# Convolution taps and modulation multiplies change places in a two-layer fp32 block on one core

## The chip, the core and the metric

One core of a Trainium2 chip runs the whole program. The metric is the device time in microseconds (us) of one execution. The engines are named as in the profile: PE (TensorE, matrix products; PEld its weight loads), DVE (VectorE), ACT (ScalarE), POOL (GpSimd) and SP (SyncE, which issues every DMA of this kernel).

## The reference

Two layers of a block with three parallel branches are computed in fp32 for 512 tokens of width 1024 and 256 context tokens; layer 1 gives the 512 tokens only.

```
mod = silu(c) @ w_mod[l] + b_mod[l]                # 6 x 1024 per token kind: sh1 sc1 g1 sh2 sc2 g2
u = x * (1 + sc1) + sh1                            # same for the context with its own columns
a, qkv, o_pre, g_if, cq, ckv, kr, gates = split(u @ w_in + b_in)
conv:   h = val * sigmoid(gate); h = depthwise_conv(h, 31 taps) + b_dw
        y_a = silu(layer_norm(h)) @ w_conv_out
mLSTM:  bidirectional chunkwise recurrence over q, k, v with gate rows g_if
        y_b = (sigmoid(o_pre) * norm(h)) @ w_mlstm_out
MLA:    attention over latent q, k, v          y_c = o @ w_mla_out
y = (g_a * y_a + g_b * y_b + g_c * y_c) @ w_out + b_out        # g_i = sigmoid(gates)
x = layer_norm(alpha * x + g1 * y)
x = layer_norm(alpha * x + g2 * (relu(u2 @ w1 + b1)^2 @ w2 + b2))      # u2 = x*(1+sc2)+sh2
```

## The kernel before

**Products.** Activations lie feature-major: 8 tiles of 128 features by T = 768 columns (512 tokens, then 256 context tokens). Each fp32 product is three float32r products, since every operand is split in a high and a low part: `wh` by `uh` (L266), `wh` by `ul` (L267) and `wl` by `uh` (L268). `gemm` makes 128 output features: 8 feature tiles by 3 matmuls over 512 columns, and the same again over the 256 of the context where they are needed (layer 0, and the keys of both layers). `win` does this for a tile of `w_in`. The PSUM tile `pg` has two buffers, `pt` four.

**Weights.** `plan` lists the weight tiles in the order of use, and `wget` keeps two tiles staged ahead. `wload` (L257 to L262) loads a tile of 512 KB into `wr`, ACT casts it to `wh` (L261), and `wl` = `wr` − `wh` is made by DVE, or by POOL for the 24 gate tiles and the 4 output gate tiles of a layer (L262). Each of the three has three buffers.

**Order of a layer.** Convolution input (4 pairs of products, value and gate, giving `hc`, L490); values with gate rows and rope keys by tokens (12 products in two halves; DVE adds the bias into `vt` L540, `gt` L543 and `kr`); the gate-row chain (ACT and DVE on 36 rows, L562 to L611), whose results PE transposes in four steps (L619) and two small products (L628); keys and queries (4 + 4 products); the mLSTM; 24 gate products, which go to DRAM (`z_dram`); 4 output gate products; the merges 0 and 1 of the branches (8 products each, reading `z_dram` back); latent products, attention, merge 2 with output projection, first norm, MLP, second norm.

**Two kinds of DVE work are spread over these products.** Python generators issue them step by step.

- `mod_pieces(l, r)` is a third of a layer's modulation. For each of 4 groups and 8 feature tiles it loads 256 KB of `w_mod` into `wm` and multiplies it into two accumulators `mda` (first tile L163, the others L165: two DVE instructions per load); then PE sums over the partitions (L173), ACT copies (L176), PE transposes (L178), DVE adds the bias (L181). `pull(k)` takes k steps. Layer 0's first third has its own code ahead of the layers; the other two are 64 steps, 128 multiplies, pulled in layer 0 beside the convolution input, values, keys and queries. Layer 1's modulation runs in layer 0's MLP and is not touched: in layer 1 the `pull`s named here find nothing left.
- `conv_taps` is the depthwise convolution: for each of 4 tiles one opening TENSOR_SCALAR (L500), then 30 steps that each add one shifted, scaled copy of `hc` to `ca` (L506). A step is one instruction over about 512 columns and, in layer 0, a second over about 256: 240 tap instructions in layer 0, 120 in layer 1. `some_taps(k)` takes k steps. Six steps are asked for after each gate product, and ahead of the convolution's layer norm, at gate product 20 in layer 0 and 21 in layer 1, the rest:

```
for b in range(3):
    for mt in range(8):
        g = gate(b, mt)
        nc.sync.dma_start(z_dram[b, mt, :, :n], g[:, :n])
        some_taps(6)
        if b * 8 + mt == (20 if l == 0 else 21):
            some_taps(200)
            ln_fm(ca, 4, groups, conv_emit)
```

`ln_fm` transposes `ca` on PE (L314), takes statistics on DVE (L315, L318) and POOL (L321), and writes the convolution's activation `sa`, which merge 0 needs.

**What sets the order.** A scheduler takes the program in the order in which it is written as a priority and fixes one static order of instructions for each engine; it may take an instruction of lower priority early where an engine would be free by its own estimate. So the taps of the text after gate products begin to run in the mLSTM. All DMAs go through SP's one queue. The tiles `wm`, `mda`, the mLSTM's `dm` and `kw`, the layer norm's `ln`, `th`, `y` and the merges' `ml` share one pool (`mw`) of 8 buffers.

Of the kernel before, what the change touches and what calls it, by code (L numbers as in the profile page):

```python
# [11 lines left out]
AF = mybir.ActivationFunctionType  # L12
# [32 lines left out]
def build(tc, I, out):  # L45
# [64 lines left out]
    # silu of the conditioning vectors, as 32 stationary columns (two of them used)  # L110
# [12 lines left out]
    def first_mod(q):  # L123
        """shift and scale of the first layer's input for 256 features"""
        wv = I["w_mod"][0].rearrange("(k p) (s q c) -> p k s q c", p=128, s=6, q=4)
        ws = []
        for k in range(8):
            w = wtile("wm")
            ws.append(w)
            nc.sync.dma_start(w.rearrange("p (s c) -> p s c", s=2), wv[:, k, 0:2, q, :])  # L130
            if not q and k == 3:
                nc.sync.dma_start(cst[:, 0:128], I["consts"][:, 0:128])
                nc.sync.dma_start(cols[0], I["cols"][0])
        yield
        ps = pt()
        for k, w in enumerate(ws):
            for t in range(4):
                PE.matmul(ps[32 * t:32 * t + 32, :128], sil[:, k, :], w[:, t * 128:(t + 1) * 128],
                          start=(k == 0), stop=(k == 7), tile_position=(0, 32 * t))
            yield  # L140
        rows = small(128, "modrows", 1)
        A.copy(rows, ps[:, :128])
        p2 = pt()
        PE.transpose(p2[:, :128], rows, ident)
        o = OFF["b_mod"]
        V.tensor_tensor(MC[0][:, 0:16, :].rearrange("p (s q t) v -> p s q t v", s=2, q=4)[:, :, q],
                        p2[:, :128].rearrange("p (s t j) -> p s t j", s=2, t=2)[:, :, :, 0:2],
                        cols[0][:, o:o + 16].rearrange("p (s q t o) -> p s q t o", s=2, q=4, o=1)[:, :, q]
                        .to_broadcast([128, 2, 2, 2]), op=OP.add)

    def mod_pieces(l, r):
        """a third of a layer's modulation: products on VectorE, paced by the matrix products, sums over
        the partitions on TensorE; the last layer's norms and gates have no context tokens"""
        nv = 1 if (l == L - 1 and r) else 2
        for g in range(4):
            av = [wtile("mda") for _ in range(nv)]
            for k in range(8):
                w = wtile("wm")
                c0 = r * 2048 + g * 512
                nc.sync.dma_start(w, I["w_mod"][l, k * 128:(k + 1) * 128, c0:c0 + 512])  # L160
                for v in range(nv):
                    if k == 0:
                        ins = V.tensor_scalar(av[v], w, sil[:, k, v:v + 1], None, op0=OP.mult)  # L163
                    else:
                        ins = V.scalar_tensor_tensor(av[v], w, sil[:, k, v:v + 1], av[v], op0=OP.mult, op1=OP.add)  # L165
                    if v == 0:
                        tc.add_manual_dep(ins.ins, mark[0].ins.name, NOSYNC)
                if k % 2 or l == 0:
                    yield
            ps = pt()  # L170
            for v in range(nv):
                for t in range(4):
                    PE.matmul(ps[32 * t:32 * t + 32, :128], pick[:, v, :], av[v][:, t * 128:(t + 1) * 128],  # L173
                              start=(v == 0), stop=(v == nv - 1), tile_position=(0, 32 * t))
            rows = small(128, "modrows", 1)
            A.copy(rows, ps[:, :128])  # L176
            p2 = pt()
            PE.transpose(p2[:, :128], rows, ident)  # L178
            i0 = r * 16 + 4 * g
            o = OFF["b_mod"] + i0  # L180
            V.tensor_tensor(MC[l][:, i0:i0 + 4, 0:nv],  # L181
                            p2[:, :128].rearrange("p (t j) -> p t j", t=4)[:, :, 0:nv],
                            cols[l][:, o:o + 4].rearrange("p (t o) -> p t o", o=1).to_broadcast([128, 4, nv]),
                            op=OP.add)
# [8 lines left out]
    def affine(l, name, g, b, sc, sh):  # L193
        """columns of (n*g + b)*(1 + sc) + sh = n*P + Q"""
# [6 lines left out]
    def plan():  # L201
        """the staged weights, in the order of their use"""
# [73 lines left out]
    # the last matrix product so far  # L276
    mark = [None]

    def gemm(w, koff, nk, act, spec):
        """psum[128 features, tokens]; w: (hi, lo) staged tiles with k tiles of 128 columns from koff;  # L280
        spec: number of tokens, or (first token, last, psum column) triples"""
# [10 lines left out]
    def gemm_parts(w, nk, act, spec):  # L292
        """as gemm, with sums of their own for every range of tokens: [(first token, last, psum)]"""
# [10 lines left out]
    def ln_groups(src, nk, groups, emit, base=0):  # L304
        """layer norm over the features of feature-major tiles; emit(k, first column, columns, psum)"""
# [50 lines left out]
    # ---------------------------------------------------------------- first modulation  # L356
# [27 lines left out]
    def first_w(j):  # L384
        """weights and sums of one of the first three products, which run along with the loads of the modulation"""
# [67 lines left out]
    for l in range(L):  # L453
# [5 lines left out]
        # token groups that follow each other through the norms: (tiles, modulation column, first token, last)  # L459
# [14 lines left out]
        # ------------------------------------------------------------ conv input  # L474
# [6 lines left out]

        for j in range(4):
            val, tg = slot("val"), slot("tg")
            for c0, c1, ps in conv_in(MT_VAL + j):
                A.activation(val[:, c0:c1], ps, AF.Identity, bias=HB(MT_VAL + j), scale=0.5)
            for c0, c1, ps in conv_in(MT_GATE + j):
                A.activation(tg[:, c0:c1], ps, AF.Tanh, bias=HB(MT_GATE + j), scale=0.5)
            pull(3)
            h = slot("hc")
            V.scalar_tensor_tensor(h[:, :n], tg[:, :n], 1.0, val[:, :n], op0=OP.add, op1=OP.mult)  # L490
            hc.append(h)
            pull(3)
# [17 lines left out]
        taps = conv_taps()  # L510
# [5 lines left out]
        # ------------------------------------------------------------ values, gates and rope keys, by tokens  # L516
# [8 lines left out]
        for hf, w_n in ((0, VG0), (1, VG1)):  # L525
            ws = [wget("w_vg", l, hf * 2 + q) for q in range(2)]
            for tt in range(NT):
# [10 lines left out]
                pull(1)  # L538
# [10 lines left out]
        # ------------------------------------------------------------ gate rows: heads forward at 0-3, backward at 32-35  # L549
# [64 lines left out]
        A.activation(E_, m, AF.Exp, scale=-1.0)  # L614
        kinds = {}
# [15 lines left out]
        # ------------------------------------------------------------ keys, queries  # L631
        kT, qT = [], []
        for h in range(MH):
            ps = win(MT_K + h, T)
            t = slot("kT")
            A.activation(t, ps, AF.Identity, bias=kb[l][:, h:h + 1], scale=KSCALE)
            kT.append(t)
            pull(4)
        for h in range(MH):
# [4 lines left out]
            pull(4)  # L644
        pull(99)

        # ------------------------------------------------------------ mLSTM
# [8 lines left out]
        def weights_of(tt, ds):  # L656
            """scores of a chunk times their decays, keys on partitions, for the directions ds"""
# [98 lines left out]
        # ------------------------------------------------------------ merges: (tanh(gate/2) + 1) * y  # L756
# [19 lines left out]
        for b in range(3):  # L776
            for mt in range(8):
                g = gate(b, mt)
                nc.sync.dma_start(z_dram[b, mt, :, :n], g[:, :n])
                some_taps(6)  # L780
                if b * 8 + mt == (20 if l == 0 else 21):
# [3 lines left out]
        # ------------------------------------------------------------ output gate of the mLSTM  # L785
        ot = []
        for h in range(MH):
# [3 lines left out]
            ot.append(t)  # L791

        def merge(b, wname, act):
            for mp2 in range(4):
                w = wget(wname, l, mp2)
                for i in range(2):
                    mt = 2 * mp2 + i
                    ps = gemm(w, 4 * i, 4, act, n)
                    for c0, c1 in segs:
# [5 lines left out]
                        nc.sync.dma_start(z_dram[b, mt, :, c0:c1], g)  # L805

        # gated, normalised mLSTM output
# [12 lines left out]
        merge(1, "w_mo", ht)  # L820

        # ------------------------------------------------------------ latent queries, keys and values
# [27 lines left out]
        def rope(x, tt, nh):  # L850
            """x: [128, nh, 32], in place"""
# [12 lines left out]
        # ------------------------------------------------------------ attention  # L864
# [164 lines left out]
        # ------------------------------------------------------------ columns of the norms and gates  # L1029
# [10 lines left out]
        # ------------------------------------------------------------ merge of the third branch, output projection  # L1040
        def packed(m):
            """m f32r tiles of 256 columns, three to a slot"""
# [22 lines left out]
        # ------------------------------------------------------------ first norm  # L1065
# [15 lines left out]
        def residual(v, c0, c1):  # L1081
            """alpha * x + g1 * b_out, two feature tiles of 256 tokens to a tile"""
# [22 lines left out]
        # ------------------------------------------------------------ MLP  # L1105
# [37 lines left out]
        # ------------------------------------------------------------ second norm  # L1143
# [49 lines left out]
def _kmaj(w, m):  # L1193
    """[K, M] -> [M/m, 128, K/128 * m]"""
# [95 lines left out]
```

## Time and profile before

| | |
|---|---|
| median of 3 runs | 2622.0 us (2621.68 to 2622.0) |
| span of the profiled execution | 2620.9 us, 38348 instructions |
| PE busy | 2482.4 us, 95% of the span |
| DVE busy | 1609.0 us, 61% |
| ACT busy | 940.4 us, 36% |
| POOL busy | 381.9 us, 15% |

No time outside the span is given for the profiled execution; its span is 1.1 us below the median of the runs. Busy times of several engines overlap. Only what keeps PE idle, or slows its clock, and what lies at the two ends lengthens a program in which PE is 95% busy: 138.5 us of the span are idle on PE. A line of the waits gives engine, tile and line that waited, then engine, tile and line that ended the wait, the sum in us, how many times, and the longest. A row of windows gives the stretch in us from the start, its length, each engine's busy time with its number of instructions, the granted clock of PE (1.00 is full speed), the share of the DMA engines and GB/s. A row of single instructions has start, duration, engine, line, operation and tiles; in brackets the time that the engine sat idle before, and who ended that.

### The profile page before, as it was taken

To read this page: it belongs to the slowest core of one execution; us is meant where nothing else is said; L and a number is where in the kernel's file an instruction comes from. 1 tells how busy PE (TensorE), PEld (TensorE's weight loads), DVE (VectorE), ACT (ScalarE), POOL (GpSimd) and SP (SyncE) were. 2 spreads that over 40 slices of the span, in tenths; PEclk is the share of its full clock that TensorE was granted. 3 is DMA by queue.
4 is the path that set the end of the run, shared out by engine and by line. 5 is a ranking of instruction groups with operands and counts; after the bars stand their busy time and mean duration, and the time that the engine had idled before them with its cause. 6 is when DMAs were issued, how large, how long until landed. Compare 5 with 4: busy or idle time off the path is not lost. (4 is left out here: it accounts for less than half of the span.)

```text
span 2620.9 us, 38348 instructions
## 1 busy us (share of the span) xinstructions
PE 2482.4 (95%) x15272; PEld 2172.9 (83%) x15272; DVE 1609.0 (61%) x2847; ACT 940.4 (36%) x1607; POOL 381.9 (15%) x235
## 2 busy tenths in 40 slices
PE   7999976999999999999999999999599999999998
PEld 5888865888897899888888989778488888988887
DVE  4887999333256777655554473489954567645456
ACT  3133311321457563222222252333133575532323
POOL 0002278303000021000000040025212000200002
PEclk9999988999999999999999999999799999999999
DMA  8543221446110554343332242224254206333333
GB/s 293 177 138 108 79 78 49 128 141 219 61 41 1 174 172 141 120 130 129 118 119 74 61 147 70 73 89 137 81 176 161 62 4 191 117 96 94 96 97 113
DMA packets 137236, 298.46 MB, mean 114 GB/s; under 512 B 13776, under 2 KB 55248, under 8 KB 137056
## 3 DMA queue, kind: packets, MB, share of 16 engines
q1 hardware_dynamic: 137056, 296.00, 35.7%
q8 instruction: 120, 1.97, 0.3%
q14 instruction: 60, 0.49, 0.1%
HBM read 265.49 MB, written 30.46 MB: 113 GB/s over the span
## 5 line engine op out<-in xcount | busy, mean ns | idle before, releaser
L261 ACT CAST wh<-wr 128x1024 fp32r<-128x1024 f32 (+1 forms) x328 | 345.6, 1055 | 1223.4 <-PE pg L267 917.7
L262 DVE TENSOR_TENSOR wl<-wr,wh 128x1024 fp32r<-128x1024 f32 (+2 forms) x272 | 340.9, 1254 | 427.0 <-ACT wh L261 423.4
L268 PE MATMUL pg<-uh,wl 128*128 128x512 f32 (+1 forms) x1280 | 457.8, 358 | 32.4 <-POOL wl L262 32.4
L266 PE MATMUL pg<-uh,wh 128*128 128x512 f32 (+1 forms) x1280 | 460.0, 359 | 1.2 <-ACT gt__17652 L760 1.2
L267 PE MATMUL pg<-ul,wh 128*128 128x512 f32 (+1 forms) x1280 | 458.7, 358 | 0.6 <-POOL ul L1167 0.6
L262 POOL TENSOR_TENSOR wl<-wr,wh 128x1024 fp32r<-128x1024 f32 x56 | 226.4, 4048 | 519.9 <-ACT wh L261 510.0
L268 PEld LDWEIGHTS pg<-uh,wl 128*128 128x128 f32 x1280 | 246.0, 192 | 65.6 <-POOL wl L262 33.7
L266 PE MATMUL pg<-hidh,wh 128*128 128x512 f32 (+1 forms) x832 | 285.8, 345 | 3.9 <-DVE mv L318 2.0
L267 PE MATMUL pg<-hidl,wh 128*128 128x512 f32 (+1 forms) x832 | 285.4, 343 | 0.0
L268 PE MATMUL pg<-hidh,wl 128*128 128x512 f32 (+1 forms) x832 | 284.4, 342 | 0.0
L266 PEld LDWEIGHTS pg<-uh,wh 128*128 128x128 f32 x1280 | 246.7, 193 | 35.5 <-ACT gt__17652 L760 1.4
L267 PEld LDWEIGHTS pg<-ul,wh 128*128 128x128 f32 x1280 | 246.3, 192 | 33.4 <-POOL ul L1167 1.1
L506 DVE SCALAR_TENSOR_TENSOR ca<-hc,cols,ca 128x511 f32<-128x511 f32 (+10 forms) x360 | 252.7, 753 | 2.4
L321 POOL TENSOR_TENSOR rs<-rs,mhalf 128x1 f32<-128x1 f32 x30 | 24.4, 819 | 1331.8 <-DVE rs L320 1299.2
L267 PE MATMUL pg<-u2l,wh 128*128 128x512 f32 (+1 forms) x608 | 210.1, 347 | 0.3 <-POOL u2l L1078 0.2
L268 PE MATMUL pg<-u2h,wl 128*128 128x512 f32 (+1 forms) x608 | 209.9, 346 | 0.0
L266 PE MATMUL pg<-u2h,wh 128*128 128x512 f32 (+1 forms) x608 | 209.7, 347 | 0.0
L1135 DVE SCALAR_TENSOR_TENSOR acc<-pg,mod,acc 128x512 f32<-128x512 f32 (+1 forms) x168 | 106.0, 659 | 168.6 <-PE pg L268 168.6
L266 PEld LDWEIGHTS pg<-hidh,wh 128*128 128x128 f32 x832 | 157.7, 190 | 25.4 <-issue 3.6
L267 PEld LDWEIGHTS pg<-hidl,wh 128*128 128x128 f32 x832 | 158.4, 190 | 18.9 <-DVE hidl L1125 1.6
L268 PEld LDWEIGHTS pg<-hidh,wl 128*128 128x128 f32 x832 | 158.1, 190 | 18.0
L165 DVE SCALAR_TENSOR_TENSOR mda<-wm,sil,mda 128x512 f32<-128x512 f32 x224 | 161.9, 748 | 3.8 <-DMA wm<-w_mod 2.2
(359 smaller groups left out, 4766.5 us busy)
## 6 DMA issues: line engine op xcount, KB each, us to landing
wr<-w SPq DMA_DIRECT2D x140, 512.0 KB, 3.6
wr<-w_in_fm SPq DMA_DIRECT2D x104, 512.0 KB, 3.6
wm<-w_mod SPq DMA_DIRECT2D x192, 256.0 KB, 4.6
wr<-w_out SPq DMA_DIRECT2D x40, 512.0 KB, 3.6
ml<-z_dram SPq DMA_DIRECT2D x104, 128.0 KB, 2.8
ml<-z_dram SPq DMA_DIRECT2D x48, 256.0 KB, 3.8
z_dram<-ml SPq DMA_DIRECT2D x32, 256.0 KB, 4.1
dm<-m_dram SPq DMA_DIRECT2D x20, 256.0 KB, 5.0
```

Source lines behind the costliest of these rows:

```text
L165: ins = V.scalar_tensor_tensor(av[v], w, sil[:, k, v:v + 1], av[v], op0=OP.mult, op1=OP.add)
L261: A.copy(h[:, :n], r[:, :n])
L262: eng.tensor_sub(lo[:, :n], r[:, :n], h[:, :n])
L266: PE.matmul(ps, hs, xh, start=first, stop=False)
L267: PE.matmul(ps, hs, xl, start=False, stop=False)
L268: return PE.matmul(ps, ls, xh, start=False, stop=last)
L321: G.tensor_tensor(rs[:, 0:1], rs[:, 0:1], mhalf[:, 0:1], op=OP.pow)
L506: V.scalar_tensor_tensor(acc[:, a:b], h[:, a + d:b + d], wd(15 + d), acc[:, a:b], op0=OP.mult, op1=OP.add)
L1135: V.scalar_tensor_tensor(acc[mt][:, c0:c1], ps[:, c0:c1], mc[:, 40 + mt, v:v + 1], acc[mt][:, c0:c1], op0=OP.mult, op1=OP.add)
```

## The change

Taps move from the gate products to the stages ahead of the mLSTM, the modulation from there to the gate products, the output gate and the merges. The generator `conv_taps` is defined ahead of the convolution input and created after the first `hc`. The key products with their code move ahead of the transposes of the gate rows. The layer norm of the convolution comes at gate product 10 in both layers. Comments and docstrings are taken out. After the change the lines are: opener L488, taps L494, `hc` L511, `vt` L541, `gt` L544, `kr` L548, gate-row transposes L628, the two small products L637.

```
 # convolution input, per pair of products
-            pull(3)
             h = slot("hc")
             V.scalar_tensor_tensor(h[:, :n], tg[:, :n], 1.0, val[:, :n], op0=OP.add, op1=OP.mult)
             hc.append(h)
-            pull(3)
+            if j == 0:
+                taps = conv_taps()
+            some_taps(9)
 # values, per product
-                pull(1)
+                some_taps(2)
 # keys: moved from behind the loop over `kinds` (the transposes) to ahead of it
+        for h in range(MH):
+            ps = win(MT_K + h, T)
+            t = slot("kT")
+            A.activation(t, ps, AF.Identity, bias=kb[l][:, h:h + 1], scale=KSCALE)
+            kT.append(t)
+            some_taps(4)
         kinds = {}
...
-            kT.append(t)
-            pull(4)
 # queries
             qT.append(t)
-            pull(4)
-        pull(99)
+            some_taps(5)
 # gates
-                some_taps(6)
-                if b * 8 + mt == (20 if l == 0 else 21):
+                some_taps(3)
+                pull(2)
+                if b * 8 + mt == 10:
                     some_taps(200)
                     ln_fm(ca, 4, groups, conv_emit)
 # output gate, per product
             ot.append(t)
+            pull(2)
 # merge, per product
                         nc.sync.dma_start(z_dram[b, mt, :, c0:c1], g)
+                    pull(2)
...
         merge(1, "w_mo", ht)
+        pull(99)
```

The static order shows where the steps end up. In the rows the names are tiles; a row is line, operation, output and inputs, and the size.

DVE in layer 0's gate stage before the change, in the middle of the taps (`ca` gets a scaled `hc`):

```order
L506 SCALAR_TENSOR_TENSOR ca<-hc,cols_82,ca 128x497
L506 SCALAR_TENSOR_TENSOR ca<-hc,cols_82,ca 128x241
L500 TENSOR_SCALAR ca<-hc,cols_82 128x768
L506 SCALAR_TENSOR_TENSOR ca<-hc,cols_82,ca 128x511
L506 SCALAR_TENSOR_TENSOR ca<-hc,cols_82,ca 128x255
```

DVE after the change, from the last mLSTM rows on into the gate stage (`mda` accumulates the modulation, `mod_99` receives its sums):

```order
L748 TENSOR_SCALAR hacc<-hacc,mmv,mrs 128x128 x4
L165 SCALAR_TENSOR_TENSOR mda<-wm,sil,mda 128x512 x10
L163 TENSOR_SCALAR mda<-wm,sil 128x512 x2
L494 SCALAR_TENSOR_TENSOR ca<-hc,cols_82,ca 128x242
L181 TENSOR_TENSOR mod_99<-pt,cols_82 128x8
L494 SCALAR_TENSOR_TENSOR ca<-hc,cols_82,ca 128x497
L494 SCALAR_TENSOR_TENSOR ca<-hc,cols_82,ca 128x241
L494 SCALAR_TENSOR_TENSOR ca<-hc,cols_82,ca 128x497
L494 SCALAR_TENSOR_TENSOR ca<-hc,cols_82,ca 128x241
L165 SCALAR_TENSOR_TENSOR mda<-wm,sil,mda 128x512 x14
L163 TENSOR_SCALAR mda<-wm,sil 128x512 x2
```

Before, 211 of layer 0's tap instructions stood behind the last mLSTM row, next to each other; now five are left there, among groups of 14 modulation multiplies. Ahead of that row stand 235 taps instead of 29, and 6 modulation multiplies instead of 128.

DVE at the first value products of layer 0 before the change:

```order
L490 SCALAR_TENSOR_TENSOR hc<-tg,val 128x768
L165 SCALAR_TENSOR_TENSOR mda<-wm,sil,mda 128x512
L163 TENSOR_SCALAR mda<-wm,sil 128x512
L165 SCALAR_TENSOR_TENSOR mda<-wm,sil,mda 128x512
L163 TENSOR_SCALAR mda<-wm,sil 128x512
L165 SCALAR_TENSOR_TENSOR mda<-wm,sil,mda 128x512
L540 TENSOR_TENSOR vt<-pg,bvg_596 128x2x128
L543 TENSOR_TENSOR gt<-pg,bvg_596 128x4x4
L540 TENSOR_TENSOR vt<-pg,bvg_596 128x2x128
L543 TENSOR_TENSOR gt<-pg,bvg_596 128x4x4
```

The same place after the change:

```order
L511 SCALAR_TENSOR_TENSOR hc<-tg,val 128x768
L488 TENSOR_SCALAR ca<-hc,cols_82 128x768
L541 TENSOR_TENSOR vt<-pg,bvg_596 128x2x128
L494 SCALAR_TENSOR_TENSOR ca<-hc,cols_82,ca 128x511
L494 SCALAR_TENSOR_TENSOR ca<-hc,cols_82,ca 128x255
```

and 12 taps further on:

```order
L494 SCALAR_TENSOR_TENSOR ca<-hc,cols_82,ca 128x508
L494 SCALAR_TENSOR_TENSOR ca<-hc,cols_82,ca 128x252
L544 TENSOR_TENSOR gt<-pg,bvg_596 128x4x4
L494 SCALAR_TENSOR_TENSOR ca<-hc,cols_82,ca 128x507
L494 SCALAR_TENSOR_TENSOR ca<-hc,cols_82,ca 128x251
L494 SCALAR_TENSOR_TENSOR ca<-hc,cols_82,ca 128x507
L494 SCALAR_TENSOR_TENSOR ca<-hc,cols_82,ca 128x251
L541 TENSOR_TENSOR vt<-pg,bvg_596 128x2x128
L544 TENSOR_TENSOR gt<-pg,bvg_596 128x4x4
```

The two additions that read the first value product stood side by side; now 16 tap instructions stand between them, and four ahead of the second product's.

PE in layer 0's keys before the change (the numbers tell buffers apart; `pg_1670` is the second key product, `cst` holds the identity):

```order
L267 MATMUL pg_1670<-ul_171,wh_1279 128x256
L268 MATMUL pg_1670<-uh_170,wl_1280 128x256
L619 MATMUL pt_1544<-cst_78,rows_1485 128x36 x6
L266 MATMUL pg_1670<-uh_178,wh_1279 128x256
L267 MATMUL pg_1670<-ul_179,wh_1279 128x256
```

and after it (`pg_1661` is the fourth key product, `pg_1773` the first query product):

```order
L267 MATMUL pg_1661<-ul_474,wh_1527 128x256
L268 MATMUL pg_1661<-uh_473,wl_1528 128x256
L628 MATMUL pt_1720<-cst_78,rows_1399 128x36 x6
L628 MATMUL pt_1730<-cst_78,lf_1410 128x36 x6
L628 MATMUL pt_1740<-cst_78,ndr_1416 128x36 x6
L628 MATMUL pt_1750<-cst_78,lnr_1414 128x36 x6
L266 MATMUL pg_1773<-uh_170,wh_1592 128x512
```

The first transposes of the gate rows, which need the end of the gate-row chain on DVE, stood inside the second key product; now all four follow the fourth. The split of the fourth key product's weights stands on DVE behind that chain.

More of the change, by code (lines that the diff above doesn't have):

```diff
@@ L480, in conv_in @@
             return [(0, n, win(i, n)[:, :n])]
[L482 to L487, printed above, removed]
-            pull(3)
-            h = slot("hc")
-            V.scalar_tensor_tensor(h[:, :n], tg[:, :n], 1.0, val[:, :n], op0=OP.add, op1=OP.mult)
-            hc.append(h)
-            pull(3)
         def conv_taps():
@@ L508, in conv_taps @@
                     yield
-        taps = conv_taps()
+        taps = None
         def some_taps(k):
@@ L514, in some_taps @@
                 next(taps, None)
+        for j in range(4):
+            val, tg = slot("val"), slot("tg")
+            for c0, c1, ps in conv_in(MT_VAL + j):
+                A.activation(val[:, c0:c1], ps, AF.Identity, bias=HB(MT_VAL + j), scale=0.5)
+            for c0, c1, ps in conv_in(MT_GATE + j):
+                A.activation(tg[:, c0:c1], ps, AF.Tanh, bias=HB(MT_GATE + j), scale=0.5)
+            h = slot("hc")
+            V.scalar_tensor_tensor(h[:, :n], tg[:, :n], 1.0, val[:, :n], op0=OP.add, op1=OP.mult)
+            hc.append(h)
+            if j == 0:
+                taps = conv_taps()
+            some_taps(9)
         vt = []
@@ L614, in build @@
         A.activation(E_, m, AF.Exp, scale=-1.0)
+        kT, qT = [], []
+        for h in range(MH):
[4 more added lines that the diff above has]
+            some_taps(4)
         kinds = {}
@@ L629, in build @@
             V.tensor_copy(ast[:, d].rearrange("p t h -> p (t h)"), ps[:, :NT * 4])
[L632 to L636, printed above, removed]
-            kT.append(t)
-            pull(4)
         for h in range(MH):
```

## The prediction, made before the changed kernel was run

> **What bounds the kernel now.** I began with the page's forty slices, which show where TensorE (PE) is not full.
>
> ```profile
> PE   7999976999999999999999999999599999999998
> DVE  4887999333256777655554473489954567645456
> POOL 0002278303000021000000040025212000200002
> PEclk9999988999999999999999999999799999999999
> GB/s 293 177 138 108 79 78 49 128 141 219 61 41 1 174 172 141 120 130 129 118 119 74 61 147 70 73 89 137 81 176 161 62 4 191 117 96 94 96 97 113
> ```
>
> A slice is 65.5 us. PE bounds the kernel almost everywhere; the holes are slices 6 and 7 (327 to 459 us, layer 0's gate products) and slice 29 (1835 to 1900 us, the same stage of layer 1), where VectorE (DVE) is full and the granted clock drops. The list of PE's waits names who ended them:
>
> ```profile
> PE pt L314 <- DVE ca L506: 37.1, 3, 22.8
> PE pg L268 <- POOL wl L262: 32.4, 3, 11.5
> PE pt L619 <- DVE rows L591: 9.6, 2, 4.9
> ```
>
> (us, times, longest.) PE waits 37.1 us for the last convolution taps in front of the convolution's layer norm, 32.4 us for gate weights whose low part GpSimd (POOL) splits off, and twice 4.8 us in the keys for the gate-row chain. The table by stage puts these on the clock:
>
> ```profile
> core 0: us, PE busy (x) PEld busy (x) DVE busy (x) ACT busy (x) POOL busy (x), PEclk, DMA share, GB/s
> 57.30:101.90 44.60, 43.98 (x277) 37.44 (x276) 35.92 (x53) 9.59 (x13) 0.00 (x0) 1.00 0.66 215
> 101.90:142.00 40.10, 39.32 (x324) 38.37 (x323) 32.86 (x83) 5.75 (x7) 0.00 (x0) 1.00 0.45 145
> 142.00:224.80 82.80, 77.72 (x496) 66.62 (x495) 65.67 (x107) 28.17 (x47) 5.88 (x3) 0.96 0.44 141
> 224.80:309.20 84.40, 78.19 (x551) 70.22 (x551) 77.52 (x209) 31.05 (x88) 15.20 (x9) 1.00 0.27 82
> 309.20:468.20 159.00, 121.89 (x656) 105.70 (x656) 144.33 (x263) 24.04 (x26) 120.69 (x15) 0.87 0.24 76
> 543.00:640.00 97.00, 97.00 (x565) 85.80 (x564) 43.50 (x60) 19.57 (x21) 18.85 (x16) 1.00 0.64 206
> 1637.40:1712.30 74.90, 70.03 (x389) 60.08 (x388) 32.78 (x56) 24.15 (x35) 7.15 (x3) 0.98 0.28 82
> 1712.30:1771.00 58.70, 52.81 (x336) 46.41 (x335) 52.20 (x130) 25.34 (x72) 10.89 (x5) 0.97 0.24 76
> 1771.00:1863.60 92.60, 92.60 (x410) 76.61 (x409) 89.39 (x110) 27.84 (x34) 48.25 (x20) 1.00 0.44 140
> 1863.60:1905.00 41.40, 9.05 (x48) 7.71 (x47) 35.69 (x57) 4.78 (x7) 4.61 (x5) 0.63 0.09 30
> ```
>
> Rows one to five are layer 0: convolution input, values, keys with queries, mLSTM, and gates up to the layer norm. Row six is the merges. The other four are layer 1's keys with queries, its mLSTM, its gates, full, and its layer norm, nearly empty: 41.40 − 9.05 = 32.35 us idle. In row five 159.00 − 121.89 = 37.1 us are idle, namely the 32.4 on POOL and 4.74 on the taps (37.1 − 32.35).
>
> Why POOL is late there:
>
> ```profile
> 354.58 26.82 POOL L262 TENSOR_TENSOR wl<-wr,wh 128x1024 fp32r<-128x1024 f32 x1 [6.54 <-ACT wh L261]
> 486.05 2.40 POOL L262 TENSOR_TENSOR wl<-wr,wh 128x1024 fp32r<-128x1024 f32 x1 [5.94 <-ACT wh L261]
> 1815.78 2.58 POOL L262 TENSOR_TENSOR wl<-wr,wh 128x1024 fp32r<-128x1024 f32 x1 [2.42 <-ACT wh L261]
> L506 DVE SCALAR_TENSOR_TENSOR ca<-hc,cols,ca 128x507 f32<-128x507 f32 (+22 forms) x43 | 22.3, 590 | 0.0
> L506 DVE SCALAR_TENSOR_TENSOR ca<-hc,cols,ca 128x497 f32<-128x497 f32 (+14 forms) x30 | 22.2, 743 | 1.0
> L165 DVE SCALAR_TENSOR_TENSOR mda<-wm,sil,mda 128x512 f32<-128x512 f32 x14 | 9.4, 743 | 0.0
> ```
>
> The same split takes 2.40 us where no taps run (second row), 26.82 us in the midst of layer 0's taps (first), and 2.58 us in the midst of layer 1's (third). Layer 0's taps come in pairs on separate columns (512 and 256), and 43 of 590 ns mean fit into 22.3 us: they overlap, 0.52 us each. Layer 1's each need the one before, 30 in 22.2 us with 1.0 us of gaps, and there POOL gets in. The Trainium skill (page "SBUF — State Buffer", section "SBUF: two separate sides") says that a VectorE operation with two SBUF inputs and a GpSimd operation that reads SBUF take turns on a shared port, each locking it for one whole instruction. By it alone a split would wait for one tap, 0.75 us at most; layer 1's 2.58 us agrees, layer 0's 26.82 us does not, so the measurement decides. By the page the first rival below could not happen and the sum would stand as it is; by the first row it keeps its chance.
>
> **The change, part by part.** Of 120 tap steps per layer 96 move ahead of the mLSTM; layer 0's 64 modulation steps (128 DVE instructions) move behind it.
>
> *Layer 0's gate stage.* No run of paired taps is left there, so 32.4 and 4.74 us of waiting go. A stalled product also restarts slowly:
>
> ```profile
> 353.40:361.75 8.35, 8.35 (x50) 7.39 (x50) 8.35 (x17) 1.85 (x2) 7.17 (x1) 1.00 0.12 47
> 370.01:388.11 18.10, 7.28 (x28) 5.61 (x27) 18.07 (x23) 1.85 (x2) 16.84 (x3) 0.72 0.31 80
> 381.46 0.80 PE L268 MATMUL pg<-uh,wl 128*128 128x512 f32 x1 [10.82 <-POOL wl L262]
> 382.05 0.63 PE L266 MATMUL pg<-uh,wh 128*128 128x512 f32 x1
> 382.48 0.63 PE L267 MATMUL pg<-ul,wh 128*128 128x512 f32 x1
> ```
>
> Behind the 10.82 us wait matmuls start 0.43 us apart, where layer 1's gates have 92.60 / 410 = 0.226. 24 of 512 columns take 5.4 us; the second row has 7.28 busy, so about 1.8 us per stall, 7.3 for the four. From above, 656 matmuls at 8.35 / 50 are 109.6 us against 121.89 busy: 12.3. Between 7.3 and 12.3 I take 9. Gain 37.1 + 9 = **46.1** (44.4 to 49.4).
>
> The modulation's multiplies that now stand there overlap too: 14 in 9.4 us (last row above), 0.67 each. A group of 16 could keep a split out for about 9.4 + 2.4 = 12 us. What a split may take before PE waits is 26.82 − 10.82 = 16 us, so I cost it at nothing; if two groups merge, see the first rival.
>
> *Layer 1's layer norm* waits for nothing any more: in the new order its last tap stands inside the mLSTM. Gain 32.35, and 2 for the clock (0.63 over 9.05 us would give 3.3): **34.3**.
>
> *Keys ahead of the gate-row transposes.* The four transposes now follow all four key products, so L619's 4.74 us and the restart (PEclk 0.96 over 77.72 us bounds it at 3.1; I take 1.5) go: 4.74 is 9.6 less layer 1's 74.90 − 70.03 = 4.87. Late next is the fourth key product: its weight split stands on DVE behind the chain, one tap opener and six taps in layer 0.
>
> ```profile
> 145.80 0.55 DVE L566 TENSOR_SCALAR ndr<-ab 36x768 f32<-36x768 f32 x1 [0.66 <-ACT ab L562]
> 164.94 0.94 DVE L611 TENSOR_TENSOR ndr<-rows,mlast 36x768 f32<-36x768 f32 x1
> L490 DVE SCALAR_TENSOR_TENSOR hc<-tg,val 128x768 f32<-128x768 f32 x4 | 3.8, 952 | 2.2 <-ACT tg L487 2.2
> L262 DVE TENSOR_TENSOR wl<-wr,wh 128x1024 fp32r<-128x1024 f32 (+2 forms) x272 | 340.9, 1254 | 427.0 <-ACT wh L261 423.4
> ```
>
> The keys start at about 142.6, the fourth at 142.6 + 3 × 8.35 = 167.65. The chain ends at 164.94 + 0.94 = 165.88; with the opener (0.95, as the 768-wide L490), 6 × 0.52 and the split's 1.25 it is 171.2. Wait 3.6, restart 1.5. Layer 0: 6.2 − 5.1 = **+1.1**. Layer 1 has two taps of 0.74 there: 165.88 + 0.95 + 1.5 + 1.25 = 169.6, a wait of 1.9 at most and hardly a restart; the gain is 4.87 + 1.5 − 1.9 = **+4.5**.
>
> *Values of layer 0.* In the new order 16 taps stand between the first product's two additions, `vt` and `gt`, and PSUM has two buffers for these products.
>
> ```profile
> 1600.10:1618.25 18.15, 18.15 (x146) 18.15 (x145) 4.68 (x13) 2.79 (x3) 0.00 (x0) 1.00 0.11 31
> L540 DVE TENSOR_TENSOR vt<-pg,bvg 128x256 f32<-128x256 f32 x8 | 3.4, 420 | 0.5 <-PE pg L537 0.5
> L543 DVE TENSOR_TENSOR gt<-pg,bvg 128x16 f32<-128x16 f32 x6 | 1.0, 165 | 0.0
> ```
>
> A product takes 18.15 / 6 = 3.03 us. The first one's buffer is free 0.42 + 16 × 0.52 + 0.17 = 8.9 us after it ends; the second product covers 3.03 of that: the third waits 5.9 us (8.3 if DVE comes late by more of the block). I take 6.5 and 1.8 for the restart: **−8.3**. It costs nothing only if the first addition comes so late that both products have to wait anyhow, or if DVE's block is done before. The seventh product has the next such place: the last `w_vg` tile's split, which needs the sixth product's first half to free its buffer, stands ahead of the fifth's `vt`: cast and split, some 2.6 us, and the additions 0.6, against 1.5 of the sixth product left: **−1.7**.
>
> *Load on DVE.* From the first convolution input to the end of layer 0's mLSTM 206 more taps and 3 openers (0.52 and 0.95: 110 us) come in, 108 multiplies and 14 openers of the modulation (0.67 and about 0.5: 79 us) go out: +31 us onto 35.92 + 32.86 + 65.67 + 77.52 = 212 busy of 251.9. So DVE has 9 us to spare plus what PE's waits add. In the mLSTM about 14 more taps, 7.3 us, meet 84.40 − 77.52 = 6.9 us of room: 0.4 to 7.3, I take **−3**. Layer 1's mLSTM has 58.70 − 52.20 = 6.5 us of room for about as many: 0 to 7, I take **−1**, since its chain waits leave PE idle anyway (52.81 of 58.70).
>
> *Modulation behind the mLSTM.* Its sums make PE wait 44.60 − 43.98 = 0.62 and 40.10 − 39.32 = 0.78 us today; they go and come back in the gates, with the layer norm's own statistics: **−0.6**. Its 64 loads move on SP's queue between the gate weights. There are 56 of them in the gates and output gates, and the other 8 fall to the first four products of the first merge, where 206 GB/s flow already. 8 × 256 KB = 2.1 MB at the 293 GB/s of the page's fastest slice are 7.2 us; 0 to 7.2, I take **−3**. In the gates 512 KB of weights and 512 KB of modulation per 8.35 us are 125 GB/s; the convolution input did 215 without a weight being late: nothing.
>
> Comments and docstrings cost nothing.
>
> **Sum.** Layer 0: 46.1 + 1.1 − 8.3 − 1.7 − 3 − 0.6 − 3 = 30.6. Layer 1: 34.3 + 4.5 − 1 = 37.8. Together 68.4. The sum is made on the profiled span of 2620.9 us, which lies 1.1 below the 2622.0 us median of the runs; 2622.0 − 68.4 gives **2554 us**.
>
> **Rivals.**
> - *The modulation locks POOL out as the taps did.* For it: 14 multiplies without a gap. Against: 12 us is below 16. If groups merge (2 × 9.4 + 2.4 = 21 us), three stalls like today's, 3 × (10.8 + 1.8) = 38, come back: 2592 us. It decides where a split exceeds 16 us.
> - *The new waits don't come.* Without values (8.3 + 1.7), mLSTM, fourth key (5.1), merge (3 each): 21 us more, 2533 us. For it: idle DVE times today would take the taps; against: the order is fixed in advance.
> - *DVE becomes the bound before the gates.* If it keeps 15% idle time as today (212 of 251.9 is 84%), its 243 us need 289, 37 us longer instead of the 18 I count there: 2573 us.
> - *Slower: gate weights behind modulation loads.* A load that waits for one of the 8 `mw` buffers blocks SP's queue, and the weights behind it. If each of 28 weight tiles came 3 us late, 84 us would outweigh 68: 2638 us; it decides from 2.5 us a tile. Against: the same mix ahead of the convolution products made PE wait 0.62 us in all.
>
> **How the numbers follow.** My sum (2541 to 2566) gets 0.53, POOL locked out 0.14, no new waits 0.14, DVE bound 0.14, slower 0.05. The range is 2532 to 2592; it leaves out the slower case and bits beyond the ends of the others. A change of 0.2% (5 us) is about what can be told from none: faster 0.92, same 0.03, slower 0.05.
>
> **What would show it.** In the changed kernel's waits, no L268 behind POOL in layer 0 and no layer norm behind a tap; gate splits under 16 us; no L628 behind the chain but one L268 behind a DVE split in the keys, 2 to 4 us; a wait of 6 us in layer 0's values, ended by `gt`; DVE over 95% busy from 57 us to the gates. I am wrong if POOL splits still last 20 us, or if PE waits for a load of `wr` in the gates.

## The result, and the profile after

The changed kernel takes 2559.0 us (median of 4 runs, 2557.35 to 2561.31), the kernel before 2622.0 (4 runs, 2621.68 to 2625.03): a ratio of 0.9757, 95% interval 0.9743 to 0.9771, 63.0 us less. The prediction was 2554 us. The profiled execution, the fastest of the four, spans 2555.5 us, 65.4 less than the one before; the prediction's sum of 68.4 was made on spans.

The forty slices of the changed kernel, as the first fence of the prediction shows them for before:

```profile
PE   7899989999999999999999999999999999999997
DVE  4999976363356777655554379996043567554456
POOL 0002132203000021000000031023411001100002
PEclk9999999999999999999999999999999999999999
```

The two holes are gone, and with them the dips of the clock; PE stands at 9 in every slice but the first and the last (7) and slices 2 and 6 (8). Of what PE still waits for, the lines that are new or have grown (us, times, longest):

```profile
PE pt L173 <- DVE mda L165: 10.3, 3, 8.0
PE pg L536 <- DVE gt L544: 6.9, 1, 6.9
PE pg L266 <- DVE ml L803: 3.6, 2, 1.9
PE pg L268 <- DVE wl L262: 2.9, 3, 2.2
```

No wait for a split on POOL, none for a tap, none for the gate rows; they made 79.1 us before. The sums of the modulation (L173) made 1.7 us before. New are the buffer that `gt` holds in the values (L536), merges that wait for a buffer's multiplication (`ml`), and the fourth key product's split. By stages of layer 0 (values; keys and queries; mLSTM with the gate products in it; gates up to the layer norm's statistics; the rest of the gates with the output gates; merges), with one row over all that stands ahead of 310 us, and then layer 1's keys with queries, and mLSTM with gates:

```profile
core 0: us, PE busy (x) PEld busy (x) DVE busy (x) ACT busy (x) POOL busy (x), PEclk, DMA share, GB/s
99.13:145.37 46.24, 39.38 (x292) 39.19 (x291) 44.12 (x112) 5.22 (x5) 0.00 (x0) 0.93 0.12 35
145.37:219.11 73.74, 71.52 (x420) 62.86 (x419) 71.70 (x124) 25.40 (x42) 8.41 (x2) 0.98 0.25 76
219.11:310.00 90.89, 83.76 (x580) 75.56 (x579) 84.80 (x224) 32.76 (x90) 17.35 (x9) 0.98 0.28 85
310.00:372.58 62.58, 54.60 (x331) 46.63 (x330) 49.23 (x96) 11.54 (x15) 22.42 (x8) 0.95 0.52 169
372.58:530.26 157.68, 152.23 (x936) 132.30 (x935) 83.98 (x126) 44.88 (x61) 40.24 (x21) 1.00 0.46 153
530.26:606.79 76.53, 72.29 (x444) 62.65 (x442) 45.98 (x74) 12.95 (x15) 15.35 (x14) 1.00 0.77 241
57.30:310.00 252.70, 236.50 (x1528) 214.66 (x1527) 239.45 (x524) 72.57 (x147) 25.75 (x11) 0.97 0.24 72
1611.54:1669.61 58.07, 58.07 (x325) 50.23 (x323) 55.12 (x78) 22.47 (x34) 4.91 (x2) 1.00 0.26 76
1669.61:1851.30 181.69, 172.75 (x906) 145.40 (x904) 95.31 (x222) 65.89 (x125) 64.03 (x32) 0.99 0.40 127
```

The same stages of before, cut at the same matrix products (keys and queries of layer 0, the merges, then layer 1's two):

```profile
142.17:221.81 79.64, 74.90 (x469) 64.67 (x467) 65.27 (x107) 25.41 (x42) 4.79 (x2) 0.96 0.45 146
559.85:629.37 69.52, 69.52 (x409) 61.61 (x408) 36.98 (x54) 12.48 (x14) 15.89 (x14) 1.00 0.73 235
1637.53:1702.62 65.09, 60.22 (x324) 51.65 (x323) 26.91 (x43) 22.71 (x34) 4.78 (x2) 0.97 0.23 69
1702.62:1912.66 210.04, 171.80 (x890) 145.35 (x889) 190.13 (x315) 64.84 (x123) 68.53 (x32) 0.92 0.31 98
```

Layer 1 gained 65.09 − 58.07 = 7.0 us in its keys and queries and 210.04 − 181.69 = 28.4 in the mLSTM and gates, with 3.0 more behind that, where the kernel before has 16 transposes of the mLSTM's output (L813) and 1.2 us of waiting; in the changed kernel these transposes lie ahead of the cut. In layer 0 the keys and queries gained 5.9 and the merges lost 7.0. DVE's 239.45 us of 252.70 ahead of the gates are 95%, where before it was busy 212 of 252.

The longest wait for the sums has a chain of its own. These rows are POOL, DVE, DVE and PE at the end of the mLSTM:

```profile
320.93 2.39 POOL L262 TENSOR_TENSOR wl<-wr,wh 128x1024 fp32r<-128x1024 f32 x1
320.99 2.41 DVE L748 TENSOR_SCALAR hacc<-hacc,mmv,mrs 128x128 f32<-128x128 f32 x1 [0.91 <-POOL mrs L746]
309.41 0.35 DVE L748 TENSOR_SCALAR hacc<-hacc,mmv,mrs 128x128 f32<-128x128 f32 x1 [0.87 <-POOL mrs L746]
337.34 0.44 PE L173 MATMUL pt<-mda,pick 128*32 128x128 f32 x4 [7.98 <-DVE mda L165]
```

A scaling of the mLSTM's norm takes 0.35 us alone and 2.41 us when a gate split has begun 0.06 us earlier. DVE came out of the mLSTM late, the modulation's next ten multiplies ran from 331.25 us on, and PE, whose order has the sums ahead of the gate products that follow, stood for 7.98 us. How much of that the gate splits make, and how much the ten multiplies (6.70 us), no run separates.

### The profile page after: what moved, and what is told of

Same layout as the page of the kernel before. It is cut to its first block, busy times and chain, and to the rows that moved or that the text cites. A ratio compares the mean times of both kernels' runs of the same rounds, so it can differ in the third digit from the quotient of the medians.

```text
span 2555.5 us, 38339 instructions
## 1 busy us (share of the span) xinstructions
PE 2470.4 (97%) x15272; PEld 2163.8 (85%) x15272; DVE 1580.6 (62%) x2847; ACT 939.5 (37%) x1607; POOL 298.7 (12%) x235
## 4 chain that ended last, share of the span: by engine, by line
PE 81%; DVE 9%; DMA 4%; ACT 2%; issue 2%; POOL 1%; SPq 0%; DVEq 0%; ACTq 0%; POOLq 0%
PE pg L266 21%; PE pg L267 21%; PE pg L268 21%; PE pt L1003 2%; PE pt L982 2%; PE pt L266 2%; PE pt L267 2%; PE pt L268 2%; DVE ca L494 2%; DMA wm<-w_mod 1%; DMA ml<-z_dram 1%; PE pg L536 1%; PE pg L538 1%; PE pg L537 1%; DVE st L315 1%
## 5 line engine op out<-in xcount | busy, mean ns | idle before, releaser
L268 PE MATMUL pg<-uh,wl 128*128 128x512 f32 (+1 forms) x1280 | 456.3, 356 | 2.2 <-DVE wl L262 2.2
L268 PE MATMUL pg<-hidh,wl 128*128 128x512 f32 (+1 forms) x832 | 284.2, 342 | 0.0
L268 PEld LDWEIGHTS pg<-uh,wl 128*128 128x128 f32 x1280 | 243.9, 191 | 34.4 <-DVE wl L262 2.7
L494 DVE SCALAR_TENSOR_TENSOR ca<-hc,cols,ca 128x511 f32<-128x511 f32 (+9 forms) x360 | 227.8, 673 | 2.4
L262 POOL TENSOR_TENSOR wl<-wr,wh 128x1024 fp32r<-128x1024 f32 x56 | 145.7, 2602 | 562.6 <-ACT wh L261 562.6
L268 PE MATMUL pg<-u2h,wl 128*128 128x512 f32 (+1 forms) x608 | 210.1, 347 | 0.0
L165 DVE SCALAR_TENSOR_TENSOR mda<-wm,sil,mda 128x512 f32<-128x512 f32 x224 | 176.2, 808 | 7.6 <-DMA wm<-w_mod 5.0
L268 PEld LDWEIGHTS pg<-hidh,wl 128*128 128x128 f32 x832 | 157.7, 189 | 18.0
```

What stands on the lines that cost most here:

```text
L262: eng.tensor_sub(lo[:, :n], r[:, :n], h[:, :n])
L268: return PE.matmul(ps, ls, xh, start=False, stop=last)
L494: V.scalar_tensor_tensor(acc[:, a:b], h[:, a + d:b + d], wd(15 + d), acc[:, a:b], op0=OP.mult, op1=OP.add)
```

## Experiments

**POOL and the taps.** The first try reordered layer 0's taps in the kernel before:

```
-                for d in [x for i in range(1, 16) for x in (-i, i)]:
-                    for s0, s1 in ((0, S), (S, n)):
+                ds = [x for i in range(1, 16) for x in (-i, i)]
+                todo_ = [(d, s0, s1) for s0, s1 in ((0, S), (S, n)) if s1 > s0 for d in ds]
+                for i, (d, s0, s1) in enumerate(todo_):
...
+                    if (i + 1) % (len(todo_) // 30) == 0:
+                        yield
```

> The kernel before, with layer 0's taps in another order: first the 30 over 512 columns, then the 30 over 256, so that nearly every tap needs the result of the one before it; number, place and result of the taps stay. Theory (overlapping, independent taps keep POOL out): the gate splits in layer 0's gate stage last under 6 us instead of 26 to 27, and PE's 32.4 us of waiting for POOL fall below 5. The taps themselves then take longer (about 1.2 us a pair instead of 1.04, 105 pairs, and some 2.4 us for each split let in), so PE's wait in front of the layer norm grows from 4.7 to some 40 to 90 us and the time may come out anywhere from 2600 to 2660. Rival (a busy DVE starves POOL however its instructions depend on each other): splits still last over 20 us and PE still waits over 25 us for POOL.

The time was 2618.1 us, ratio 0.9984 (0.9974 to 0.9994), and PE still waited 34.7 us for POOL, as the rival says. But the edit had not done what it was for: in the static order the scheduler let one tile's taps over 256 columns alternate with the next tile's over 512, so neighbours were independent again. The POOL row and the DVE row of the first long split:

```profile
349.91 28.43 POOL L262 TENSOR_TENSOR wl<-wr,wh 128x1024 fp32r<-128x1024 f32 x1 [5.31 <-ACT wh L261]
375.67 2.95 DVE L505 SCALAR_TENSOR_TENSOR ca<-hc,cols,ca 128x248 f32<-128x248 f32 x2
```

The split ends at 378.34, 2.2 us behind the first place at which two dependent taps stood side by side (the pair of the second row, with a gap of 0.036 us between them at 376.14). So the order was pinned:

```
                     ins = V.scalar_tensor_tensor(acc[:, a:b], ...)
+                    if l == 0:
+                        tc.add_manual_dep(ins.ins, prev[0].ins.name, NOSYNC)
+                    prev[0] = ins
```

> As the run with chained taps, but now the order is pinned: in layer 0 each tap is kept behind the one before it, so that two tiles' chains no longer alternate, and every tap needs the result of its neighbour. In the first run POOL got in exactly where two dependent taps stood next to each other. Theory (POOL gets in at the 0.036 us gap ahead of a dependent tap): all gate splits in layer 0's tap stretch under 6 us, PE's 34.7 us of waiting for POOL under 5; the taps' stretch gets about 25 us (dependent taps) and 2 us for each split longer, so the wait in front of the layer norm takes it back: time between 2600 and 2650. Rival (a busy DVE starves POOL in any case): splits over 20 us again and over 25 us of waiting.

The gate splits between 330 and 460 us, and the taps there, in the kernel before and then in this one:

```profile
L262 POOL TENSOR_TENSOR wl<-wr,wh 128x1024 fp32r<-128x1024 f32 x11 | 113.1, 10303 | 22.8 <-ACT wh L261 22.8
L506 DVE SCALAR_TENSOR_TENSOR ca<-hc,cols,ca 128x503 f32<-128x503 f32 (+14 forms) x206 | 117.8, 644 | 0.1
...
L262 POOL TENSOR_TENSOR wl<-wr,wh 128x1024 fp32r<-128x1024 f32 x15 | 38.1, 2537 | 87.5 <-ACT wh L261 87.5
L510 DVE SCALAR_TENSOR_TENSOR ca<-hc,cols,ca 128x500 f32<-128x500 f32 (+19 forms) x157 | 123.0, 785 | 5.4
```

A split takes 2.54 us in the mean, the longest 2.84, and PE does not wait for POOL's splits any more. DVE is about as busy as before: its idle time between taps grew from 0.1 us to 5.4, in gaps of 0.036. So what shuts POOL out is a run of VectorE instructions that overlap, not a busy VectorE. The time is 2625.3 us, ratio 1.0012 (1.0001 to 1.0023): PE's waits in front of the layer norms went from 37.1 us to 64.4 (layer 0's share from 4.7 to 32.1), and those of the norms' second transposes from 3.9 to 15.8. Letting POOL in gains nothing while the taps stay where they are.

In the kernel before, the trace shows a second way in, without a gap. Three of its four long splits end 2.3 us after a tap opener (L500) begins, and these openers take 2.69 to 2.72 us, where one with no split beside it takes 0.67; the fourth ends 2.2 us behind the last tap. Why an opener lets POOL in is not shown.

**Each layer, each part.** Layer 0 as before and layer 1 as changed (conditions on the layer around the same calls):

> Layer 0 ordered as in the kernel before, layer 1 as in the changed kernel. The prediction's share of layer 1 is 37.8 us: 2584 us. The traces of before and after put 39.4 us behind layer 1's values: 2582. Rival (part of layer 1's gain came from layer 0's order, such as weights that are ahead): 2590 or more.

2583.8 us, ratio 0.9851 (0.9834 to 0.9867): 38.4 us from layer 1, without layer 0's help. Layer 0's waits stay what they were, and of the waits for taps only layer 0's is left:

```profile
PE pg L268 <- POOL wl L262: 32.4, 3, 11.5
PE pt L314 <- DVE ca L494: 4.8, 1, 4.8
```

Next, the kernel before with only the keys moved, in both layers:

```
+        for h in range(MH):
+            ps = win(MT_K + h, T)
...
         kinds = {}
```

> The kernel before, with only the key products moved ahead of the gate-row transposes. By the prediction's terms: 1.1 us in layer 0 and 4.5 in layer 1, 5.6 together, 2616 us; PE's 9.6 us of waiting for the rows go, a wait of 2 to 4 us for the fourth key's split comes in each layer. Rival (layer 1's keys and queries took 7.0 us less in the changed kernel, so the fourth key's split costs nothing there and the restart costs more than 1.5): 10 to 12 us, about 2611.

2613.5 us, ratio 0.9973 (0.9963 to 0.9984): 8.3 us, between the two. Keys and queries, layer 0 and 1:

```profile
144.06:222.82 78.76, 73.99 (x470) 63.89 (x467) 64.98 (x107) 25.51 (x42) 4.79 (x2) 0.98 0.46 148
1637.09:1695.16 58.07, 58.07 (x324) 50.21 (x323) 26.84 (x43) 22.23 (x34) 4.79 (x2) 1.00 0.26 78
```

Layer 1 gains the whole 7.0 us: no wait at all for the fourth key's split. Layer 0 gains 79.64 − 78.76 = 0.9: a modulation sum waits 4.8 us there in place of the rows.

Taps early, but the modulation left where it was:

```
             some_taps(9)
+            pull(3)
...
-                pull(2)
```

> The changed kernel, with layer 0's modulation back beside the convolution input, values, keys and queries, so that taps and modulation both run there. Theory (DVE has some 9 us of room there and gets about 79 us more): PE waits 50 to 70 us more ahead of layer 0's gates, the sums' waits of 10 us and the merges' 5 us go, and the time is about 2615 us (2600 to 2630). Rival (only the taps' leaving counted, DVE is not full): 2545 us, 14 below the changed kernel.

2601.2 us, ratio 0.9922 (0.9902 to 0.9942). Its convolution input, values, and keys with queries:

```profile
57.30:116.80 59.50, 50.28 (x291) 41.57 (x290) 58.54 (x100) 10.44 (x14) 0.00 (x0) 0.91 0.41 130
116.80:182.59 65.79, 44.27 (x330) 41.26 (x328) 65.29 (x126) 8.00 (x11) 0.00 (x0) 0.84 0.38 121
182.59:282.88 100.29, 80.78 (x465) 67.42 (x466) 89.44 (x158) 21.85 (x33) 21.80 (x2) 0.88 0.34 110
```

DVE is busy 213 of 225.6 us, and in the first two stages for all but 1.5: it has become the bound there. The queries end at 282.88 instead of 219.11, 63.8 us late, inside the forecast; the time lies at the low end of it. Once the taps stand early, taking the modulation out of their way is worth 2601.2 − 2559.0 = 42.2 us. What its move would be worth with the taps in their old place no run shows.

**The new waits.** Modulation from the seventh gate product on, three steps each, none in the merges:

```
-                pull(2)
+                if b * 8 + mt >= 6:
+                    pull(3)
```

> The changed kernel, with layer 0's modulation pulled three steps per gate product from the seventh on and three per output gate product, none in the first gate products and none in the merges. Theory (the first sum stood on PE at a point where DVE was still busy with the mLSTM's end, and the merges' loads met the modulation's): the 8.0 us wait of the first sum and its restart of about 1.8 go, and some 4 us of the merges: about 2545 us. Rival (DVE and DMA are as late at the later places; the waits only move): 2555 to 2562.

2546.7 us, ratio 0.9718 (0.9701 to 0.9734), 12.3 us below the changed kernel. The sums' waits and the merges:

```profile
PE pt L173 <- DVE mda L165: 2.6, 3, 1.6
525.41:596.11 70.70, 70.70 (x427) 61.99 (x426) 37.81 (x57) 12.63 (x15) 16.15 (x14) 1.00 0.74 237
```

Merges of 70.70 us instead of 76.53 are 5.8; by the profiles 4.9 more came ahead of the merges, which begin at 525.41 instead of 530.26. Next the value products' order, in the changed kernel:

```
-            some_taps(9)
+            some_taps(9 if j < 3 else 3)
...
-                some_taps(2)          # ahead of the additions vt, gt
+                some_taps(2)          # behind them
```

> The changed kernel, with three instead of nine tap steps after the fourth pair of the convolution input and the two steps of a value product placed behind its additions, so that gt stands right behind vt; six tap steps more are left for the later stages. Theory (the 6.9 us wait of the third value product comes from the 16 taps between the two additions alone): it goes, and with it some 6 us: about 2553 us. Rival (DVE's backlog passes on to the keys' splits and the mLSTM): 2557 to 2560.

2551.2 us, ratio 0.9728 (0.9713 to 0.9742): 7.8 us. The values take 37.5 us instead of 46.2, and the fourth key's wait is 0.3 us, which makes 11.4 us by the end of the queries. A third of it is lost again: the second transposes of the layer norm wait 8.1 us, behind a DVE that worked off the six tap steps among the modulation's multiplies. Both edits:

> The two edits together: modulation later, and the value order. Theory (two places, independent): 12.3 + 6 us below the changed kernel's 2559, about 2541 us. Rival (six more tap steps in the mLSTM delay the first modulation sum again): 2546 or more.

2547.1 us, ratio 0.9711 (0.9696 to 0.9725): the rival's side. The two do not add up, and the prediction's first rival came true here, with taps and multiplies mixed:

```profile
PE pg L268 <- POOL wl L262: 9.8, 1, 9.8
319.47 30.43 POOL L262 TENSOR_TENSOR wl<-wr,wh 128x1024 fp32r<-128x1024 f32 x3 [2.98 <-ACT wh L261]
```

Taps that were left over and modulation multiplies stood without a gap from 317 to 343 us. The row covers three splits; the first of them, from 319.47 on, took 25.8 us by itself, and PE waited 9.8. So the leftover was moved into the queries (besides the line shown, the modulation begins one gate product later, with four steps per output gate product):

```
-            some_taps(5)
+            some_taps(7)
```

> The run with both edits, with seven instead of five tap steps after each query product, and the modulation from the eighth gate product on (three steps per gate product, four per output gate product): fewer taps are left behind the mLSTM, where in the run with both edits taps and modulation stood together without a gap for about 25 us and one split kept PE waiting 9.8 us. Theory (that gap-free run locked POOL out, and shorter runs let it in before PE needs the split): no wait for POOL, 9.8 us and a restart of about 1.5 less, some of it lost again to more taps in the mLSTM: about 2538 us (2534 to 2542). Rival (the taps have no free place in front of the gates; the mLSTM becomes longer by the same amount): 2546 or more.

2547.3 us, ratio 0.9713 (0.9697 to 0.9729): again the rival's. The wait for POOL is gone, and the mLSTM has it instead:

```profile
PE pt L694 <- DVE dm L672: 11.3, 5, 5.4
```

So POOL's wait was not what held the two edits together at 2547.1 us. The three versions (modulation later, both edits, this one) agree within 0.6 us, and the waits change place. That DVE's work ahead of the layer norm, which stays what it is, sets this time is an argument from these waits; no run takes that work away. Of the versions run these are the fastest.

## Why the prediction was right, point by point

- *Layer 0's gate stage, 46.1.* The waits were right. The 37.1 us went: no L268 behind POOL, no layer norm behind a tap. The clock's share of 9 can't be read alone. From the queries' end to the gates' end the stages shrank by 304.7 − 276.9 = 27.8; 37.1 less the sums' 9.6, 1.7 more of the norm's waits, 1.0 more of the mLSTM's, and some 3 for the four sums more that stand there (about 0.7 us each) leaves about 6 for it, below the 7.3 to 12.3 of the prediction.
- *The rivals on POOL.* In the changed kernel the splits there last 2.4 us by the median. The modulation kept one of them out for 5 us: begun at 347.89 us inside a group of multiplies, it took 7.4, short of the 12 that the prediction gave for a group, and PE did not wait. That the multiplies can cost PE time, once taps stand among them, the run with both edits shows: its split of 25.8 us is 9.8 beyond the 16 that the prediction gave as the point, and PE waited just these 9.8. With the modulation left ahead of the gates PE waited 8.8 us for a split as well.
- *Layer 1, 37.8.* Right: 38.4 by itself, and 7.0 + 28.4 + 3.0 = 38.4 in the profiles. Mechanism and waits are as said; the keys gave 7.0 for 4.5, since the wait of up to 1.9 us for the fourth split did not come, and mLSTM with gates gave 31.4 for 34.3 − 1.
- *Keys of layer 0, +1.1.* Right in kind: the wait moved to the fourth key's split, 2.2 us where 3.6 was said. The stage gained 5.9, since three of the modulation's sums left it as well, which the sum books elsewhere.
- *Values, −8.3 and −1.7.* The first wait is 6.86 us where 5.9 to 8.3 was the range and 6.5 taken, ended by `gt`. The wait at the seventh product did not come. From 40.3 us the stage grew to 46.2, by 6 instead of 10; two of the modulation's sums left it.
- *Load on DVE.* 239.45 us against 212 + 31 = 243, and 95% busy as forecast; the mLSTM's waits grew by 1.0 us instead of 3. With the modulation left there too, DVE was the bound.
- *Modulation behind the mLSTM, −0.6 and −3.* Here the sum failed. The sums' waits were 7.98 and 1.67 in the gates, for 1.40 in the conv stages before: about −8, and more with the restart. The prediction took the price from the old place and overlooked that the first group now stands behind the mLSTM's norm on DVE, which the gate splits themselves hold up. The merges lost 7.0, not 3: 3.6 are waits for `ml`, 0.6 is a wait for a sum, some 1.4 are two sums that moved in, and the rest can't be told apart. It was inside the bounds of 0 to 7.2, at the end. The loads were the reason given; the run that took the modulation out of the merges took loads and multiplies out together, so which of them delayed `ml` stays open.
- *The total.* 68.4 was forecast on the spans and 65.4 came, and that they lie so close is partly luck. Up to the end of layer 0's queries 2.7 us were gained where a loss of 8.9 was forecast; from there to the merges 26.9 instead of 42.5; the merges lost 7.0 instead of 3; layer 1 gave 38.4 for 37.8. The errors are +11.6, −15.6, −4.0 and +0.6; a part of the first two is the sums' own time on PE, which moved from one stage to the other. Another 1.0 us lies in layer 1's attention, where nothing was changed, and 3.4 between the latent products and layer 1, where nothing was changed either, yet the stage took 898.9 us instead of 902.3. Nearly all of the 3.4 lies where PE's waits are the same and the granted clock is not, before and after:

```profile
697.67:763.00 65.33, 63.60 (x336) 58.83 (x335) 23.65 (x67) 28.09 (x43) 1.33 (x1) 0.95 0.15 44
675.09:737.40 62.31, 60.42 (x337) 56.33 (x335) 23.82 (x67) 28.26 (x43) 1.33 (x1) 1.00 0.15 46
```

The eleven profiles show that the change is not the reason. From the first product of this stretch to the first transpose behind it (L978 before) seven of them take 64.2 us at a clock of 1.00, among them the kernel before with only the keys moved; two take 65.8 at 0.97, and two, the kernel before and the one with layer 1 alone, 67.4 at 0.95.

The Trainium skill (page "TensorE: Matmul & The Clock Gate", section "Part 1: The HAM clock gate") says that the gate watches windows that run freely, so that the same kernel has another number of slow matmuls at its start from run to run. The eleven profiles agree in kind, in the middle of a kernel; why the clock fell in four of them was not tried. The single runs of one version lie 1 to 8 us apart.

## What to carry to other kernels

Where a weight split or another job of GpSimd sits beside a long run of VectorE work, ask whether that run has a gap: here a chain of dependent instructions left one, pairs of independent ones did not, and GpSimd then waited for the end of the run. A stage that has room on the list of busy shares has it only until the work moved there is counted: work has to go out before other work comes in. Price a moved wait by its new neighbours (who is late on that engine at that moment), not by what it cost in its old place.

## What the runs showed of the hardware that was not expected

- VectorE instructions that overlap keep a GpSimd operation out for as long as their run lasts: 26.82 and 28.43 us here over some 50 instructions of 0.45 to 0.74 us. One gap of 0.036 us ahead of a dependent instruction let it in, and in the kernel before so did a tap opener without a gap. With a gap ahead of nearly every tap, 15 of 15 splits took 2.84 us or less.
- It works the other way too: a split of 2.4 us that had begun 0.06 us earlier stretched a VectorE instruction of 0.35 us to 2.41, and so a share of VectorE's time goes to GpSimd's work.
